# Attention heads of a diffusion trunk: one maximum per query over all keys, unscaled probabilities, sums divided out in the output projection, and no GpSimd work in the heads

## The chip, the cores and the metric

The kernel runs on one core of a Trainium2 chip. Times are device microseconds (us) of one execution. The engines are TensorE (PE; its weight loads are PEld), VectorE (DVE), ScalarE (ACT), GpSimd (POOL) and SyncE (SP, which only issues DMAs here). Each runs its own queue in order and waits on semaphores for the others. PSUM, into which TensorE writes, has eight banks of 128 partitions by 512 fp32 values.

## The reference, cut to what matters

Two layers over 256 context tokens and 1024 latent tokens, each with a token mixer and an MLP. Layer 0 mixes by latent attention with 8 heads, and the change is there:

```python
def mla_attend(q_nope, q_rope, k_nope, k_rope, v):
    scale = (MLA_NOPE + MLA_ROPE) ** -0.5
    s = (jnp.einsum('bqhd,bkhd->bhqk', q_nope, k_nope, preferred_element_type=jnp.float32)
         + jnp.einsum('bqhr,bkr->bhqk', q_rope, k_rope, preferred_element_type=jnp.float32))
    p = jax.nn.softmax(s * scale, axis=-1)
    return jnp.einsum('bhqk,bkhd->bqhd', p.astype(v.dtype), v)
...
    o_lat = jnp.moveaxis(o_lat, 0, 1).reshape(B, S, MLA_HEADS * MLA_V)
    y_lat = o_lat @ w_o
    ...
        o_ctx = mla_attend(q_nope[:, :C], q_rope[:, :C], k_nope[:, :C], k_rope[:, :C], v[:, :C])
        y_ctx = o_ctx.reshape(B, C, MLA_HEADS * MLA_V) @ w_o
```

Latent queries read all 1280 keys, context queries the 256 context keys. Layer 1 (gated linear attention) and the two MLPs are as before.

## The kernel before

Everything is fp32. A product of two fp32 operands is made of three fp32r matmuls: each operand is split into a high part (a cast on ACT, `split`, L203, or `evac`, L575) and the low rest (a subtraction, `sub`, L200, on DVE or POOL); `mm3` (L233 to L235) issues hi*hi, hi*lo, lo*hi.

Tokens are in three blocks: block 0 is the context (256), blocks 1 and 2 are latent (512 each). `heads` runs over 8 heads, and in each over five chunks of 256 queries: two of block 1, two of block 2, one of block 0. For each chunk:

- `scores` (L688) takes two tiles of 128 queries. For each tile it makes the scores against each block of keys in turn (blocks 1, 2 and 0, five matmuls each, L706 to L710), takes that block's maximum on DVE (L711), and exponentiates with that maximum on ACT (L713), with the row sum in the same instruction. The scores against block 0 of both tiles share one PSUM tile, `last`. Then the three maxima are brought together: their minimum (negated maxima, L718), three correction factors by an exponential on ACT (L719), the total (L720), its reciprocal (L722), the factors times it (L723), and each block of probabilities is scaled by its factor (L725): on DVE, but for the first tile's block 1, which is scaled on POOL (`PLAN['sc']`).
- `transposes` (L729) turns the probabilities of the chunk before (TensorE, L738) and splits them. For the pairs of key tiles at 2 and 4 (`PLAN['raw']`) the split goes through an SBUF copy on ACT (L741), so that POOL can do the subtraction; the other three go straight from PSUM, with the subtraction on DVE.
- `attend` multiplies the chunk before that one with the values (L233 to L235, 256 columns each) and stores the result in the DRAM tensor `o_scr`.

Between these, `PLAN` lays out pieces of other work: the next head's keys, queries and rotary parts (`items`), and the modulation vectors (`ada`): `ada_near` as one multiply-and-sum on DVE (L252), `ada_far` as a multiply on POOL (L249) and a sum on ACT (L250). The weights of the heads are split with the subtraction on POOL, and so is one multiply of `rope` (L568).

After the heads `out_proj` multiplies `o_scr` by `w_o`, block 1 first, then 0, then 2, in two halves of the outputs. In the first half each step of k loads a head's `o_scr` rows and splits them with the subtraction on DVE. The residual and norm of the block before run beside it on DVE and ACT (`residual_norm_steps`, L859 and L861).

The builder's scheduler sets each engine's order: it starts from the order of the program text and moves instructions by its own estimate of when they are ready. Loads whose tile is `ada` in the heads are pinned.

Of the kernel before, what the change touches and what calls it, by code (L numbers as in the profile page):

```python
# [14 lines left out]
ALU = mybir.AluOpType  # L15
# [56 lines left out]
 'sc': [(0, 1)],  # L72
 'raw': [4, 2],
# [37 lines left out]
class Trunk:  # L111
    def __init__(self, ctx, tc, I, out, stop=None):
# [35 lines left out]
        self.o_scr = dram("o_scr", [HEADS, P, T])  # L148
        self.hid_scr = [dram(f"hid{l}", [NP, 7, P, 512]) for l in range(2)]
# [409 lines left out]
    def rope(self, raw, b, w):  # L559
        nc, I = self.nc, self.I  # L560
        if b == 0:
            return raw
        c = slice(BLK[b][0] - CTX, BLK[b][0] - CTX + w)
        cos, sin = self.load(I["cos"][:, c], "t"), self.load(I["sin"][:, c], "t")
        sh = self.t(w)
        nc.vector.stream_shuffle(out=sh, in_=raw, mask=SHUF)
        nc.vector.tensor_tensor(out=raw, in0=raw, in1=cos, op=ALU.mult)
        nc.gpsimd.tensor_tensor(out=sh, in0=sh, in1=sin, op=ALU.mult)  # L568
        nc.vector.tensor_tensor(out=raw, in0=raw, in1=sh, op=ALU.add)
        return raw  # L570
# [32 lines left out]
    def hweight(self, h, n):  # L603
        if n not in self.hw:
            self.hw[n] = self.weight(self.I[n][h])
# [33 lines left out]
    def v_items(self, p):  # L639

        self.wv = self.weight(self.I["wv"][p])
# [15 lines left out]
    def heads(self):  # L657
# [3 lines left out]
        for h in range(HEADS):  # L661
            nxt = self.head_items(h + 1) if h + 1 < HEADS else iter(())
            for ci, c in enumerate(((1, 0), (1, 256), (2, 0), (2, 256), (0, 0))):
                pt = self.scores(self.st[h], c)
                for x in PLAN['order'][ci].split():
# [8 lines left out]
                    if x == "ada":  # L674
                        self.ada_some(self.ada_near, PLAN['near'][h][ci], pinned=True)
                        self.ada_some(self.ada_far, PLAN['far'][h][ci], pool=True, pinned=True)
# [9 lines left out]
        self.ada_some(self.ada_far, 1000, pool=True)  # L686

    def scores(self, st, c):  # L688
# [7 lines left out]
        res = []  # L696
        for i in range(2):
            qs = slice(o + i * P, o + i * P + P)
            mx, rs, ex, f = (self.tiny(4) for _ in range(4))
            p = {}  # L700
            for n, kb in enumerate(keys):
# [10 lines left out]
                p[kb] = self.m(w)  # L712
                nc.scalar.activation(p[kb], ps, AF.Exp, bias=mx[:, n:n + 1], accum_out=rs[:, n:n + 1])  # L713
            k = len(keys)
            if k == 1:
                nc.vector.reciprocal(out=f[:, 0:1], in_=rs[:, 0:1])
            else:
                nc.vector.tensor_reduce(out=mx[:, 3:4], in_=mx[:, 0:3], axis=AX.X, op=ALU.min)  # L718
                nc.scalar.activation(ex[:, 0:3], mx[:, 0:3], AF.Exp, bias=mx[:, 3:4], scale=-1.0)  # L719
                nc.vector.tensor_tensor_reduce(out=f[:, 0:3], in0=ex[:, 0:3], in1=rs[:, 0:3], scale=1.0, scalar=0.0,  # L720
                                               op0=ALU.mult, op1=ALU.add, accum_out=f[:, 3:4])
                nc.vector.reciprocal(out=ex[:, 3:4], in_=f[:, 3:4])  # L722
                nc.vector.tensor_scalar(out=f[:, 0:3], in0=ex[:, 0:3], scalar1=ex[:, 3:4], scalar2=None, op0=ALU.mult)  # L723
            for n, kb in enumerate(keys):
                (nc.gpsimd if (i, kb) in PLAN['sc'] else nc.vector).tensor_scalar(out=p[kb], in0=p[kb], scalar1=f[:, n:n + 1], scalar2=None, op0=ALU.mult)  # L725
            res.append(p)
        return res

    def transposes(self, p, c):  # L729
        nc = self.nc  # L730
        res = []
        for j in range(0, 2 if c[0] == 0 else NT, 2):
# [6 lines left out]
            if j in PLAN['raw']:  # L739
                raw = self.t()  # L740
                nc.scalar.copy(raw, ps)  # L741
                res.append(self.msplit(raw))
            else:
                res.append(self.evac(ps, 512))
# [50 lines left out]
    def out_items(self, res, l, b, wname, src, off, xsrc):  # L795
# [867 lines left out]
```

## Time and profile before

| what | value |
|---|---|
| time, median of 3 runs | 2922.29 us (2915.41 to 2922.88) |
| profiled execution | 2915.37 us, span in its trace 2913.6 us |
| TensorE busy | 2746.1 us (94%) |
| VectorE busy | 2313.1 us (79%) |
| ScalarE busy | 1603.9 us (55%) |
| GpSimd busy | 664.0 us (23%) |
| granted TensorE clock over the span | 0.971 |

The span is from the first to the last instruction of the trace. Busy shares are means over stages with different limits, so the parts below look at the heads (182 to 710 us of the span) and at the output projection (710 to 862 us) by themselves. Matmuls overlap in the pipeline: the time of one is longer than the step from one to the next, and the step from start to start is what it costs.

### The profile page before, as it was taken

How to read it: one execution, taken by the hardware profiler on the slowest of the kernel's cores; microseconds unless marked ns; L12 is line 12 of the kernel's file. 1: busy time of each engine (PE TensorE's matmuls, PEld its weight loads, DVE VectorE, ACT ScalarE, POOL GpSimd, SP SyncE). 2: the span in 40 equal slices, each digit the busy share in tenths (PEclk: the TensorE clock that was granted, in tenths of full speed). 3: DMA queues.
4: the chain of work that ended last, by engine and by line, in shares of the span. 5: the costliest groups of instructions: out<-in, count | busy, mean ns of one | idle time of the engine just before them, and what ended most of it. 6: DMA issues, size and time to landing. Idle time of an engine off the chain costs nothing. (4 is left out here: it accounts for less than half of the span.)

```text
span 2913.6 us, 44354 instructions
## 1 busy us (share of the span) xinstructions
PE 2746.1 (94%) x14646; PEld 2354.7 (81%) x14646; DVE 2313.1 (79%) x4331; ACT 1603.9 (55%) x3360; POOL 664.0 (23%) x474
## 2 busy tenths in 40 slices
PE   6799998999989999999999999799888999999997
PEld 4678887898779888888887888688887778888877
DVE  8898899888788887798868673366898898877666
ACT  4566666666466444444545365656665644545443
POOL 5554444422000000000002233356561000000012
PEclk8999999999999999999999999899999999999999
DMA  5222424313646675498735465666586657677454
GB/s 201 77 77 67 129 94 143 101 61 110 230 124 233 197 250 179 163 342 285 245 122 172 166 222 161 202 218 230 189 275 213 224 195 246 203 269 259 146 178 154
DMA packets 319383, 535.47 MB, mean 184 GB/s; under 512 B 33072, under 2 KB 96432, under 8 KB 319152
## 3 DMA queue, kind: packets, MB, share of 16 engines
q1 hardware_dynamic: 313328, 527.39, 54.5%
q10 hardware_dynamic: 5760, 5.25, 0.5%
q8 instruction: 115, 1.88, 0.3%
q14 instruction: 116, 0.95, 0.1%
q0 software_dynamic: 64, 0.00, 0.0%
HBM read 412.18 MB, written 120.32 MB: 183 GB/s over the span
## 5 line engine op out<-in xcount | busy, mean ns | idle before, releaser
L234 PE MATMUL ps<-m,w 128*128 128x512 f32 (+1 forms) x2320 | 897.5, 388 | 13.2 <-DVE m L200 13.2
L233 PE MATMUL ps<-m,w 128*128 128x512 f32 (+1 forms) x2320 | 882.2, 390 | 25.2 <-ACT m L203 14.5
L235 PE MATMUL ps<-m,w 128*128 128x512 f32 (+1 forms) x2320 | 889.7, 387 | 2.1 <-DVE w L200 2.0
L200 POOL TENSOR_TENSOR w<-stg,w 128x512 fp32r<-128x512 f32 (+2 forms) x138 | 194.1, 1409 | 1706.2 <-ACT w L203 1648.3
L233 PEld LDWEIGHTS ps<-m,w 128*128 128x128 f32 x2320 | 439.4, 190 | 118.8 <-ACT m L203 21.8
L234 PEld LDWEIGHTS ps<-m,w 128*128 128x128 f32 x2320 | 442.0, 191 | 103.8 <-DVE m L200 18.3
L235 PEld LDWEIGHTS ps<-m,w 128*128 128x128 f32 x2320 | 440.1, 190 | 91.6 <-DVE w L200 4.4
L203 ACT CAST w<-stg 128x512 fp32r<-128x512 f32 (+2 forms) x510 | 311.1, 615 | 333.0 <-PE ps L234 247.2
L200 DVE TENSOR_TENSOR w<-stg,w 128x512 fp32r<-128x512 f32 x372 | 273.1, 738 | 142.6 <-ACT w L203 127.8
L203 ACT CAST m<-stg 128x512 fp32r<-128x512 f32 x296 | 177.5, 625 | 141.8 <-DMA stg<-hid 123.6
L233 PE MATMUL ps<-m,m 128*128 128x256 f32 (+1 forms) x632 | 187.9, 316 | 28.7 <-ACT m L203 17.7
L200 DVE TENSOR_TENSOR m<-stg,m 128x512 fp32r<-128x512 f32 x244 | 169.1, 706 | 50.0 <-ACT m L203 49.2
L234 PE MATMUL ps<-m,m 128*128 128x256 f32 (+1 forms) x632 | 198.0, 315 | 7.4 <-DVE m L200 4.1
L233 PE MATMUL ps<-c,w 128*128 128x256 f32 (+1 forms) x664 | 186.9, 288 | 15.8 <-ACT c L435 6.3
L235 PE MATMUL ps<-m,m 128*128 128x256 f32 (+1 forms) x632 | 194.9, 310 | 2.4 <-DVE m L426 2.4
L234 PE MATMUL ps<-c,w 128*128 128x256 f32 (+1 forms) x664 | 185.8, 284 | 5.6 <-DVE c L436 3.5
L235 PE MATMUL ps<-c,w 128*128 128x256 f32 (+1 forms) x664 | 185.1, 284 | 0.6 <-DVE w L200 0.6
L233 PEld LDWEIGHTS ps<-m,m 128*128 128x128 f32 x632 | 124.0, 197 | 39.8 <-ACT m L203 19.7
L203 ACT CAST w<-m 128x512 fp32r<-128x512 f32 x128 | 79.2, 622 | 117.1 <-PE ps L234 116.9
L233 PEld LDWEIGHTS ps<-c,w 128*128 128x128 f32 x664 | 125.7, 192 | 21.2 <-ACT c L435 6.7
L888 DVE TENSOR_TENSOR t<-ps,t 128x512 f32<-128x512 f32 x164 | 111.0, 684 | 37.6 <-PE ps L235 27.1
L234 PEld LDWEIGHTS ps<-m,m 128*128 128x128 f32 x632 | 125.2, 198 | 17.6 <-POOL m L200 5.5
(303 smaller groups left out, 5817.5 us busy)
## 6 DMA issues: line engine op xcount, KB each, us to landing
stg<-in_mlp_w SPq DMA_DIRECT2D x256, 256.0 KB, 4.2
stg<-hid SPq DMA_DIRECT2D x227, 256.0 KB, 3.8
hid<-t SPq DMA_DIRECT2D x205, 256.0 KB, 3.3
stg<-in_w SPq DMA_DIRECT2D x182, 256.0 KB, 3.4
ada<-in_adaT SPq DMA_DIRECT2D x88, 512.0 KB, 3.7
stg<-in_adaT SPq DMA_DIRECT2D x112, 256.0 KB, 4.1
stg<-in_gla_wv SPq DMA_DIRECT2D x64, 256.0 KB, 3.6
stg<-in_mla_wo SPq DMA_DIRECT2D x48, 256.0 KB, 4.4
```

The lines of the kernel that those rows point to most:

```text
L200: eng.tensor_tensor(out=out, in0=a, in1=bits(hi), op=ALU.subtract)
L203: self.nc.scalar.copy(hi, src)
L233: mm(ps, lhs[0], rhs[0], start=first, stop=False, skip_group_check=shared)
L234: mm(ps, lhs[0], rhs[1], start=False, stop=False, skip_group_check=shared)
L235: mm(ps, lhs[1], rhs[0], start=False, stop=last, skip_group_check=shared)
L888: eng.tensor_tensor(out=out, in0=a, in1=b, op=op)
```

## The change

`scores` first makes all scores of a query tile, then takes one minimum of the negated maxima, and only then exponentiates all blocks with it. The row sums go into two small constant tiles per head, `parts` and `whole`. Nothing scales the probabilities. A new function `head_sums` adds the sums of a head, takes the reciprocals, turns them with one transpose on TensorE and stores 1280 numbers in a DRAM tensor `f_scr`; it is called for head h - 1 after the second chunk's scores of head h, and for the last head behind all scores. `out_proj` loads, beside each head's `o_scr` rows, the row of `f_scr` broadcast to all partitions, and multiplies on DVE before the split. In the heads the subtractions of the weights and of all transposed probabilities, the multiply of `rope` and the `ada_far` products move from POOL to DVE; the copies for `PLAN['raw']` go.

```diff
@@ rope
-        nc.gpsimd.tensor_tensor(out=sh, in0=sh, in1=sin, op=ALU.mult)
+        nc.vector.tensor_tensor(out=sh, in0=sh, in1=sin, op=ALU.mult)
@@ hweight, v_items
-            self.hw[n] = self.weight(self.I[n][h])
+            self.hw[n] = self.weight(self.I[n][h], self.nc.vector)
-        self.wv = self.weight(self.I["wv"][p])
+        self.wv = self.weight(self.I["wv"][p], self.nc.vector)
@@ heads
+                self.st_of = h
                 pt = self.scores(self.st[h], c)
+                if ci == 1 and h:
+                    self.head_sums(h - 1)
...
-                        self.ada_some(self.ada_far, PLAN['far'][h][ci], pool=True, pinned=True)
+                        self.ada_some(self.ada_far, PLAN['far'][h][ci], pinned=True)
...
         self.attend(*prev)
+        self.head_sums(HEADS - 1)
         self.attend(*later[:2], self.transposes(*later[2:]), later[3])
@@ scores
                 nc.vector.tensor_reduce(out=mx[:, n:n + 1], in_=ps, axis=AX.X, op=ALU.max, negate=True)
-                p[kb] = self.m(w)
-                nc.scalar.activation(p[kb], ps, AF.Exp, bias=mx[:, n:n + 1], accum_out=rs[:, n:n + 1])
...
+                pss.append(ps)
+            top = mx[:, 0:1]
+            if len(keys) > 1:
+                top = mx[:, 3:4]
+                nc.vector.tensor_reduce(out=top, in_=mx[:, 0:3], axis=AX.X, op=ALU.min)
             for n, kb in enumerate(keys):
-                (nc.gpsimd if (i, kb) in PLAN['sc'] else nc.vector).tensor_scalar(out=p[kb], in0=p[kb], scalar1=f[:, n:n + 1], scalar2=None, op0=ALU.mult)
+                p[kb] = self.m(BLK[kb][1])
+                acc = whole[:, j:j + 1] if len(keys) == 1 else parts[:, j - 2, n:n + 1]
+                nc.scalar.activation(p[kb], pss[n], AF.Exp, bias=top, accum_out=acc)
...
+    def head_sums(self, h):
+
+        nc = self.nc
+        parts, whole = self.sums[h % 2]
+        nc.vector.tensor_reduce(out=whole[:, 2:NT], in_=parts, axis=AX.X, op=ALU.add)
+        nc.vector.reciprocal(out=whole, in_=whole)
+        ps = self.ps(P)
+        nc.tensor.transpose(ps[0:NT], whole, self.ident)
+        y = self.t(P)
+        nc.scalar.copy(y[0:NT], ps[0:NT])
+        nc.scalar.dma_start(self.f_scr[h].rearrange("(j t) -> j t", t=P), y[0:NT])
@@ transposes
-            if j in PLAN['raw']:
-                raw = self.t()
-                nc.scalar.copy(raw, ps)
-                res.append(self.msplit(raw))
-            else:
-                res.append(self.evac(ps, 512))
+            res.append(self.evac(ps, 512))
@@ out_items (out_proj)
                 if half == 0:
-                    o.append(self.msplit(self.load(src[k, :, t0 - off:t0 - off + w]), w, self.nc.vector))
+                    x = self.load(src[k, :, t0 - off:t0 - off + w])
+                    if l == 0:
+                        f = self.load(self.f_scr[k:k + 1, t0:t0 + w].to_broadcast([P, w]))
+                        self.tt(self.nc.vector, x, x, f, ALU.mult)
+                    o.append(self.msplit(x, w, self.nc.vector))
```

The change moves instructions in the heads, in the output projection, and in a few places just ahead of them and at the start of the first MLP; behind that every engine's order is the same as before. Two places matter below. Names such as `ps_5380` are tiles with their number; the same tile has another number in the other program.

The first is on ACT, in the last latent chunk of the fifth head (`scores` L713 before, L726 now; L719 are the correction factors, L575 and L741 evacuate transposes). Before:

```order
L713 ACTIVATE c_5743,y_5716<-ps_5714,y_5715 128x256
L713 ACTIVATE m_5726,y_5716<-ps_5719,y_5715 128x512
L713 ACTIVATE m_5735,y_5716<-ps_5728,y_5715 128x512
L719 ACTIVATE y_5717<-y_5715 128x3
L713 ACTIVATE m_5764,y_5754<-ps_5757,y_5753 128x512
L713 ACTIVATE m_5773,y_5754<-ps_5766,y_5753 128x512
L575 CAST m_5830<-ps_5825 128x512
L713 ACTIVATE c_5781,y_5754<-ps_5714,y_5753 128x256
```

Now:

```order
L726 ACTIVATE m_5259,parts_98<-ps_5238,y_5237 128x512
L726 ACTIVATE m_5261,parts_98<-ps_5245,y_5237 128x512
L726 ACTIVATE c_5263,parts_98<-ps_5236,y_5237 128x256
L762 COPY t_5324<-ps_5293 128x256
L764 DMA o_scr<-t_5324 128x256
L726 ACTIVATE m_5287,parts_98<-ps_5266,y_5265 128x512
L726 ACTIVATE m_5289,parts_98<-ps_5273,y_5265 128x512
L726 ACTIVATE c_5291,parts_98<-ps_5236,y_5265 128x256
L575 CAST m_5332<-ps_5327 128x512
L726 ACTIVATE c_5388,whole_99<-ps_5380,y_5381 128x256
```

The three exponentials of a query tile now stand together behind the tile's last maximum, and the evacuation of the first transposes (`m_5332`) and the first exponential of the context chunk (`c_5388`) stand behind the second tile's three.

The second place is on TensorE, in the context chunk that follows in the same head. Its two score groups go into the two halves of one PSUM tile (`ps_5882` before, `ps_5380` now); the rows lead up to the second group. L233 to L235 are `attend`, L738 (L751 now) transposes. Before (ahead of these rows stand the first group and four matmuls of `attend`):

```order
L234 MATMUL ps_5911<-m_5831,m_5186 128x256
L235 MATMUL ps_5911<-m_5830,m_5187 128x256
L738 MATMUL ps_5945<-ident,c_5743 128x128 x2
L738 MATMUL ps_5954<-ident,m_5726 128x128 x2
L738 MATMUL ps_5965<-ident,m_5726 128x128 x2
L738 MATMUL ps_5976<-ident,m_5735 128x128 x2
L738 MATMUL ps_5954<-ident,m_5764 128x128 x2
L738 MATMUL ps_5965<-ident,m_5764 128x128 x2
L738 MATMUL ps_5976<-ident,m_5773 128x128 x2
L233 MATMUL ps_5911<-m_5841,m_5203 128x256
L738 MATMUL ps_5945<-ident,c_5781 128x128 x2
L706 MATMUL ps_5882<-c_4418,c_4976 128x256
```

Now, from the last matmul of the second latent tile's scores on:

```order
L716 MATMUL ps_5236<-k_1174,m_4406 128x256
L751 MATMUL ps_5363<-ident,m_5093 128x128 x2
L751 MATMUL ps_5363<-ident,m_5121 128x128 x2
L712 MATMUL ps_5380<-c_4074,c_4568 128x256
L713 MATMUL ps_5380<-c_4075,c_4568 128x256
L714 MATMUL ps_5380<-c_4074,c_4569 128x256
L715 MATMUL ps_5380<-k_1173,c_4552 128x256
L716 MATMUL ps_5380<-k_1174,c_4552 128x256
L233 MATMUL ps_5399<-m_5332,m_4751 128x256
L751 MATMUL ps_5433<-ident,c_5263 128x128 x2
L751 MATMUL ps_5433<-ident,c_5291 128x128 x2
L712 MATMUL ps_5380<-c_4074,c_4568 128x256
```

Between the two groups of the context chunk stood 7 matmuls of `attend` and 16 transposes; now one matmul of `attend` and four transposes stand there. So it is in heads 1, 3, 5, 7 and 8 of the 8 now; in heads 2, 4 and 6 more stands between.

## Rows read from the trace of the kernel before

**Rows 1.** Busy time of each engine by stage: start:end, length, busy (instructions), clock, DMA.

```profile
182.00:710.00 528.00, 503.26 (x3265) 455.98 (x3264) 466.66 (x1101) 349.46 (x904) 226.10 (x145) 0.97 0.29 94
758.00:780.00 22.00, 22.00 (x174) 21.17 (x173) 18.53 (x34) 13.32 (x25) 0.00 (x0) 1.00 0.50 146
780.00:800.00 20.00, 14.04 (x62) 11.25 (x62) 20.00 (x36) 11.09 (x22) 0.00 (x0) 0.74 0.75 262
```

**Rows 2.** Waits of TensorE in the heads: us in total, times, longest.

```profile
PE ps L233 <- DVE m L200: 5.6, 2, 2.8
PE ps L706 <- DVE m L579: 4.3, 4, 1.9
PE ps L706 <- DVE m L200: 3.2, 1, 3.2
PE ps L738 <- DVE m L725: 2.9, 1, 2.9
```

**Rows 3.** Timeline of DVE around one of these waits: start, us, instruction.

```profile
461.64 2.59 DVE L725 TENSOR_SCALAR m<-m,y 128x512 f32<-128x512 f32 x1
...
465.96 2.07 DVE L723 TENSOR_SCALAR y<-y 128x3 f32<-128x3 f32 x1
```

**Rows 4.** Timeline of POOL in the same stretch.

```profile
459.18 4.76 POOL L249 TENSOR_TENSOR ada<-ada,cs 128x1024 f32<-128x1024 f32 x2 [9.23 <-DVE y L722]
...
465.63 2.38 POOL L249 TENSOR_TENSOR ada<-ada,cs 128x1024 f32<-128x1024 f32 x1
```

**Rows 5.** DVE's groups in the heads: count, busy us, mean ns, idle before.

```profile
L200 DVE TENSOR_TENSOR m<-ps,m 128x512 fp32r<-128x512 f32 x134 | 89.9, 681 | 20.4 <-ACT m L575 15.5 <-PE ps L234 3.5 <-PE ps L235 0.9
L252 DVE CUSTOM_DVE_ANT_0 ada<-ada,cs 128x1024 f32<-128x1024 f32 x48 | 66.0, 1376 | 0.0
L725 DVE TENSOR_SCALAR m<-m,y 128x512 f32<-128x512 f32 x96 | 59.1, 642 | 2.3
L725 DVE TENSOR_SCALAR c<-c,y 128x256 f32<-128x256 f32 x80 | 46.1, 577 | 0.3
L723 DVE TENSOR_SCALAR y<-y 128x3 f32<-128x3 f32 x64 | 31.4, 490 | 0.7
...
L718 DVE TENSOR_REDUCE y<-y 128x1 f32<-128x3 f32 x64 | 9.4, 146 | 0.4
```

**Rows 6.** POOL's groups in the heads.

```profile
L200 POOL TENSOR_TENSOR m<-t,m 128x512 fp32r<-128x512 f32 x64 | 84.9, 1346 | 86.3 <-ACT m L203 45.0 <-PE ps L235 14.8 <-PE ps L738 7.8
L249 POOL TENSOR_TENSOR ada<-ada,cs 128x1024 f32<-128x1024 f32 x24 | 57.4, 2398 | 28.4 <-DMA ada<-in_adaT 15.7 <-DVE y L722 9.2 <-ACT m L203 2.3
...
L200 POOL TENSOR_TENSOR w<-stg,w 128x384 fp32r<-128x384 f32 (+2 forms) x18 | 18.0, 1002 | 23.8 <-ACT w L203 23.8
```

**Rows 7.** Timeline of ACT where it waits for nothing, early in the heads.

```profile
194.28 0.68 ACT L713 ACTIVATE m<-ps,y 128x512 f32<-128x512 f32 x1
...
194.95 0.58 ACT L575 CAST m<-ps 128x512 fp32r<-128x512 f32 x1
195.41 0.49 ACT L713 ACTIVATE c<-ps,y 128x256 f32<-128x256 f32 x1
...
195.87 0.31 ACT L719 ACTIVATE y<-y 128x3 f32<-128x3 f32 x1
```

**Rows 8.** Timeline of TensorE where it waits for nothing, in the heads.

```profile
403.70 1.91 PE L738 MATMUL ps<-ident,m 128*128 128x128 f32 x16
405.36 0.48 PE L706 MATMUL ps<-m,m 128*128 128x512 f32 x1
...
407.76 0.28 PE L706 MATMUL ps<-c,m 128*128 128x256 f32 x1
407.88 0.28 PE L707 MATMUL ps<-c,m 128*128 128x256 f32 x1
```

**Rows 9.** Timeline of DVE in the output projection, block 2's first half.

```profile
790.59 1.28 DVE L200 TENSOR_TENSOR m<-stg,m 128x512 fp32r<-128x512 f32 x2
791.79 0.69 DVE L861 TENSOR_TENSOR m<-m,s 128x512 f32<-128x512 f32 x1
```

More of the change, by code (lines that the diff above doesn't have):

```diff
@@ L71 @@
          [1, 0, 4, 0, 1], [0, 1, 2, 0, 0]],
- 'sc': [(0, 1)],
- 'raw': [4, 2],
  'bufs': {'m': 37, 'c': 16, 'w': 8, 'stg': 1, 't': 5, 'ada': 3},
@@ L148, in __init__ @@
         self.o_scr = dram("o_scr", [HEADS, P, T])
+        self.f_scr = dram("f_scr", [HEADS, T])
+        self.sums = [(const(f"parts{i}", [P, NT - 2, 3]), const(f"whole{i}", [P, NT])) for i in range(2)]
         self.hid_scr = [dram(f"hid{l}", [NP, 7, P, 512]) for l in range(2)]
@@ L683, in heads @@
         self.attend(*prev)
+        self.head_sums(HEADS - 1)
         self.attend(*later[:2], self.transposes(*later[2:]), later[3])
         self.ada_some(self.ada_near, 1000)
-        self.ada_some(self.ada_far, 1000, pool=True)
+        self.ada_some(self.ada_far, 1000)
     def scores(self, st, c):
@@ L696, in scores @@
         res = []
+        parts, whole = self.sums[self.st_of % 2]
         for i in range(2):
+            j = (BLK[qb][0] + o) // P + i
             qs = slice(o + i * P, o + i * P + P)
-            mx, rs, ex, f = (self.tiny(4) for _ in range(4))
-            p = {}
+            mx = self.tiny(4)
+            pss, p = [], {}
             for n, kb in enumerate(keys):
@@ L711, in scores @@
                 nc.vector.tensor_reduce(out=mx[:, n:n + 1], in_=ps, axis=AX.X, op=ALU.max, negate=True)
-                p[kb] = self.m(w)
-                nc.scalar.activation(p[kb], ps, AF.Exp, bias=mx[:, n:n + 1], accum_out=rs[:, n:n + 1])
-            k = len(keys)
-            if k == 1:
-                nc.vector.reciprocal(out=f[:, 0:1], in_=rs[:, 0:1])
-            else:
[L718 to L723, printed above, removed]
+                pss.append(ps)
[3 more added lines that the diff above has]
+                nc.vector.tensor_reduce(out=top, in_=mx[:, 0:3], axis=AX.X, op=ALU.min)
             for n, kb in enumerate(keys):
-                (nc.gpsimd if (i, kb) in PLAN['sc'] else nc.vector).tensor_scalar(out=p[kb], in0=p[kb], scalar1=f[:, n:n + 1], scalar2=None, op0=ALU.mult)
+                p[kb] = self.m(BLK[kb][1])
+                acc = whole[:, j:j + 1] if len(keys) == 1 else parts[:, j - 2, n:n + 1]
+                nc.scalar.activation(p[kb], pss[n], AF.Exp, bias=top, accum_out=acc)
             res.append(p)
         return res
+    def head_sums(self, h):
[8 more added lines that the diff above has]
+        nc.scalar.dma_start(self.f_scr[h].rearrange("(j t) -> j t", t=P), y[0:NT])
     def transposes(self, p, c):
@@ L738, in transposes @@
                     nc.tensor.transpose(ps[:, jj * 256 + i * P:jj * 256 + i * P + P], p[i][b][:, o:o + P], self.ident)
-            if j in PLAN['raw']:
-                raw = self.t()
-                nc.scalar.copy(raw, ps)
-                res.append(self.msplit(raw))
-            else:
-                res.append(self.evac(ps, 512))
+            res.append(self.evac(ps, 512))
         return res
```

## The prediction

> **What bounds the kernel now.** I read first the table of stages, because the change touches two of them alone. In the heads, 182 to 710 us, TensorE is busy 503.3 of 528.0 us and its granted clock is 0.97 [rows 1]. So two things are there to be won: 528.0 - 503.3 = 24.7 us in which TensorE has nothing to run, and what the lower clock costs. A mean of 0.97 between the levels 2.4 and 1.2 GHz means that 6% of the stage ran at the lower one, where each step takes twice its time; 3% of 528 is about 16 us. Together 41 us is the most that this stage can give, since the change takes no matmul away (it adds 8 transposes).
>
> Next the waits of TensorE there: the four longest, 16.0 of the 24.7 us, all end with DVE, at subtractions (L200, L579) and at a scaling (L725) [rows 2]. DVE is busy 466.7 of 528.0 us, 88% [rows 1], which alone is no full engine. The timeline says why it is late. At 461.64 a scaling takes 2.59 us, and at 465.96 a TENSOR_SCALAR on 128x3 numbers takes 2.07 us [rows 3]; each ends with a POOL multiply: the pair that starts at 459.18 ends at 463.94, the next, from 465.63, at 468.01 [rows 4], while the scaling ends at 464.23 and the small one at 468.03. Over the stage the operation on three numbers takes 490 ns in the mean [rows 5], more than three times the reduction of three numbers beside it (146 ns). So DVE stands still behind POOL's longer instructions, a piece of the evacuation comes late, TensorE runs dry, and the clock falls: where TensorE is busy throughout, 758 to 780, it is 1.00, and where it idles for 6 of 20 us, 0.74 [rows 1]. The reader is to see that DVE is short of time in stretches, through POOL.
>
> **What the change takes from the heads.** The scalings on DVE (59.1 + 46.1 us) and the factors (31.4 us) go [rows 5], 136.6 us, and some smaller operations of the old correction with them. To DVE come 64 subtractions, whose POOL copies take 84.9 us there, 24 `ada` products and 18 weight subtractions [rows 6]. At DVE's own prices [rows 5]: 64 x 0.681 = 43.6; 24 x 1.376 = 33.0 at most, as that mean is stretched by POOL too; 18 x 0.681 = 12.3 at most, for most are narrower. With 7 multiplies of `rope` at the same 0.68 (4.8 us) and 8 calls of `head_sums`, bounded by 0.15 and 0.7 us for each of its two operations (2 to 11 us, I take 3, since one has 10 numbers and the other 24 a row), 97 us are added. So DVE loses 40 us or more in a stage that now gives PE its waits, the stretching of the rest goes with POOL, and its share falls under 81%. ACT, at 349.5 us of 528 [rows 1], only loses work (copies, factors, the `ada` sums).
>
> What remains of the 41 us cannot be read from a row. Below, it could be nothing, if other waits end just behind the ones removed; above, all of it. The waits that the trace names end with DVE, and DVE gets both less to do and even durations, so I take four fifths of both parts: 20 us of idle and 12 us of clock, **-32 us**.
>
> **What it adds to the heads.** One maximum over all keys makes the exponentials wait for the tile's last scores. Before, the exponential of a block stood right behind its own maximum; now three stand together, and their PSUM tiles are kept until then. Most chunks have cover: by the new order, with each step at the price of rows 8, TensorE has some 7 us of `attend`, transposes and items between the two tiles' last scores [rows 8], and a tile's maximum, minimum and three exponentials need under 4. The context chunk has not. The prices are: an exponential of 512 columns with its sum 0.67 us (194.28 to 194.95), a cast 0.46 (to 195.41), one of 256 columns 0.46 (to 195.87) [rows 7]; the reduction over three numbers 0.146 [rows 5]; a maximum over 256 columns I take at 0.4, between the 0.146 of that and the 0.681 of an operation twice as wide [rows 5]. From the end of the second latent tile's last scores to the end of the context chunk's first exponential ACT then needs 0.4 + 0.15 + 0.67 + 0.67 + 0.46 + 0.46 + 0.46 = 3.3 us, and the second half of `ps_5380` cannot be written before that, as both halves share one tile. TensorE gets there after 8 transposes at (405.36 - 403.70) / 16 = 0.104 us and 6 matmuls of 256 columns at 0.12 us [rows 8]: 1.6 us. It waits 1.7 to 1.8 us. In this order that is so in five heads of eight: **+9 us**. Before, 2.5 us of matmuls and transposes stood between the two groups alone, and the exponential came at once, so nothing was lost. Below, this is nothing, if TensorE gets there late anyway; above, the same wait at all 40 chunks would be 70 us (it is the second rival).
>
> The 8 transposes of the sums and their copies are below 0.2 us each on TensorE and under other work.
>
> **What it adds to the projection.** 24 multiplies on DVE and 24 loads. A subtraction of 512 columns costs 0.60 us from start to start ((791.79 - 790.59) / 2 [rows 9]); the multiply has the same form, so 16 x 0.60 and 8 of half the width at about 0.33 (an estimate between half and the whole of 0.60) make 12 us. Block 1 comes first, where TensorE has 2.8 us of work for each step (12 steps of 0.23, twice the 0.12 of half the columns [rows 8]) and DVE three operations, 1.8 us: hidden, but for about 1 us at the start, as the second step's factor is now loaded, multiplied, cast and subtracted before TensorE can go on. In block 0 a step is 1.4 us on TensorE and 0.33 + 0.33 + 0.60 on DVE, beside the norm of block 1; DVE is busy 18.5 of 22.0 us there [rows 1], so its 3.5 idle us take the 2.6 us with little over: 1 us. In block 2 there is no cover: from 780 to 800 DVE is busy 20.00 of 20.00 us, TensorE 14.04 at a clock of 0.74 [rows 1]; its 8 x 0.60 = 4.8 us come on top, with about 1 us of lower clock. Sum **+8 us**; 0 if all hides, 14 if nothing does. The loads go on SP's queue between the others; the DMA share there is 0.50 to 0.75 [rows 1], so they have room. The last head's `f_scr` row is only wanted in the eighth step.
>
> **The sum.** -32 + 9 + 8 = -15 us on the profiled execution's 2915.4 gives 2900. That execution stands 6.9 us under the median of the runs shown; against 2922.3 the same difference gives **2907 us**.
>
> **A rule weighed.** The stage's own rows say that DVE loses 40 us net. The Trainium skill, "Perfetto Trace Analysis", section "Optimizing Scalar/DVE Operations", speaks against the direction: where DVE is saturated, it suggests moving work off it, to ScalarE or even GpSimd, and adds that the shared port may make the latter useless. Here DVE is at 88% and the change moves POOL's work to it. Had the scalings stayed, the sum by that rule would be 467 + 97 = 564 us of DVE in a stage of 528, a bound of +36 us.
>
> **The rivals.** First, *all of it is won*: the context chunk's wait is covered by TensorE's own lateness and the stage comes near its matmuls. -38 + 3 + 5 = -30, 2892 us. For it: every wait of rows 2 ends with DVE. Against: the order above has too little between the two groups. Chance 0.17.
>
> Second, *the joint maximum costs as much as POOL did*. Each of the 32 latent chunks loses 0.5 us as well, because exponentials wait behind casts on ACT or PSUM tiles come free late: -15 + 16 = +1, 2923 us. For it: ACT holds the casts of the transposes behind the exponentials. Against: ACT is busy two thirds of the stage. Chance 0.27.
>
> Third, *slower*: scores of two chunks meet in PSUM. A chunk holds five of the eight banks until its second tile's exponentials are done, and the next chunk wants five. If a chunk must wait the 1.3 us that a second tile's maximum, minimum and first exponential take (0.4 + 0.15 + 0.67), 32 x 1.2 = 38 us go: -15 + 38 = +23, 2945 us. It decides from 24 / 32 = 0.75 us for each chunk on, where the loss passes 9 us. Against: TensorE has transposes and `attend` that need no new bank from the held ones. Chance 0.10.
>
> Fourth, *DVE stays the bound* by the moved work, as in the rule: TensorE's waits come of DVE's sheer load in stretches where few scalings stood, so nothing of the 32 us is won, and a tenth of the added 97 us falls into such stretches: +9 + 8 + 10 = +27, 2949 us. Against: the durations of rows 3, which are POOL's. Chance 0.05.
>
> **How the numbers follow.** My forecast has 0.41. A measurement of this kernel tells 0.3%, 8.8 us, from no change. Faster by more than that: nearly all of the forecast (0.38) and of the first rival (0.17): 0.55. Within: the second rival and the rest of the forecast: 0.30. Slower: the third and fourth, 0.15. The forecast's own range is 2897 to 2917. The range reaches from a little past the first rival, 2886, with nearly the whole 41 us, to 2930, past the second rival and a first part of the third, and leaves out no more than 0.2.
>
> **What would show it.** Right: DVE's TENSOR_TENSOR and `ada` operations in the heads keep to one duration; TensorE's idle there falls from 24.7 to under 15 us, and what is left stands at the first matmul of the second context group, released by ACT; the clock of the stage is 0.99. Between the end of the heads and the first MLP's steady run the stage is about 8 us longer, with DVE full in block 2. Wrong: waits of the scores' first matmuls for ACT in every chunk (second or third rival), or DVE idle-free over long stretches of the heads (fourth).

## The result and the profile after

The changed kernel takes 2969.89 us in the median of 4 runs (2962.81 to 2972.21) against 2920.83 us before (4 runs on the same chip), a ratio of 1.0167 with a 95% interval of 1.0144 to 1.0189. The forecast was 2907 us and a gain; the change loses some 49 us. The profiled execution took 2962.81 us, its span is 2961.0 us.

To compare stages of kernels whose heads differ in length, the heads are taken here from the first score matmul to the first matmul of the output projection, and the projection from there to the first store of the next stage's `hid`. First these two stretches before, then after (columns as in [rows 1]: start:end, length, busy of PE, PEld, DVE, ACT and POOL, clock, DMA share, GB/s):

```profile
176.11:716.38 540.27, 512.08 (x3314) 463.17 (x3312) 473.66 (x1108) 356.79 (x919) 232.37 (x150) 0.97 0.29 94
716.38:854.49 138.11, 128.96 (x632) 108.25 (x632) 108.34 (x196) 77.56 (x145) 0.00 (x0) 0.95 0.63 206
```

```profile
176.79:758.44 581.65, 522.86 (x3321) 465.79 (x3319) 394.88 (x818) 285.36 (x750) 2.87 (x2) 0.97 0.27 87
758.44:904.73 146.29, 130.44 (x632) 108.77 (x632) 120.12 (x218) 76.90 (x145) 0.00 (x0) 0.93 0.71 232
```

The heads are 41.4 us longer and the projection 8.2 us. What lies behind both is 2913.6 - 854.5 = 2059.1 us before and 2961.0 - 904.7 = 2056.3 us after. In the heads every engine but TensorE has less to do, DVE 79 us less, and still TensorE's idle time rises from 540.3 - 512.1 = 28.2 us to 58.8 us. So no engine is short of time over the stage; something comes late. The waits of TensorE in the heads, which answer to [rows 2] (total us, times, longest), say who is waited for:

```profile
PE ps L712 <- ACT m L726: 10.5, 9, 1.6
PE ps L233 <- ACT m L726: 9.6, 4, 5.1
PE ps L751 <- ACT m L726: 9.3, 10, 1.6
PE ps L712 <- DVE m L579: 8.2, 3, 3.6
PE ps L233 <- ACT c L726: 5.4, 3, 1.8
```

Before, the four longest ended with DVE. Now four of the five longest end with ACT's exponentials (L726), at the first matmul of a score group (L712), at the transposes (L751) and at other products. ACT itself is busy 285.4 of 581.6 us. Its groups in the heads (columns as in [rows 5]) show what it waits for: DVE's minimum, L722, with 130.9 us of idle time ahead of the wide exponentials.

```profile
L726 ACT ACTIVATE m<-ps,y 128x512 f32<-128x512 f32 x128 | 86.8, 684 | 132.3 <-DVE y L722 130.9 <-ACT t L762 0.4 <-DVE y L717 0.4
```

And DVE's groups there, which answer to [rows 5], show that the minimum in turn stands behind TensorE: 72.8 us of DVE's idle time lie ahead of the maxima over 256 columns, those of the context keys, and end with the last matmul of a score group, L716.

```profile
L252 DVE CUSTOM_DVE_ANT_0 ada<-ada,cs 128x1024 f32<-128x1024 f32 x72 | 87.5, 1216 | 4.4 <-DMA ada<-in_adaT 4.4
...
L717 DVE TENSOR_REDUCE y<-ps 128x1 f32<-128x256 f32 x80 | 33.5, 418 | 82.4 <-PE ps L716 72.8 <-PE ps L751 9.6
...
L722 DVE TENSOR_REDUCE y<-y 128x1 f32<-128x3 f32 x64 | 9.6, 149 | 0.9
```

So TensorE waits for ACT, ACT for DVE, and DVE for TensorE's context scores. The loop can be seen in one chunk. The rows are TensorE's timeline in the last head (start, us, instruction, idle before it). The first row starts the first query tile's context scores, written into the shared tile `last`; the third starts the second query tile's, into the other half of the same tile, 7.1 us later; the last starts the next chunk's scores.

```profile
707.30 0.28 PE L712 MATMUL ps<-c,m 128*128 128x256 f32 x1
...
712.53 0.66 PE L751 MATMUL ps<-ident,m 128*128 128x128 f32 x4 [0.89 <-ACT m L726]
...
714.41 0.36 PE L712 MATMUL ps<-c,m 128*128 128x256 f32 x1
...
716.84 0.50 PE L712 MATMUL ps<-m,m 128*128 128x512 f32 x1 [1.15 <-ACT m L726]
```

ACT's timeline of the same stretch. The first row opens the first tile's exponentials; its third exponential, from 713.04, is the one that reads `last` and ends at 713.51. Only then may the other half be written, and TensorE does so 0.9 us later, at 714.41. The last row opens the second tile's.

```profile
711.70 0.69 ACT L726 ACTIVATE m<-ps,y 128x512 f32<-128x512 f32 x1 [0.77 <-DVE y L722]
...
713.04 0.47 ACT L726 ACTIVATE c<-ps,y 128x256 f32<-128x256 f32 x1
...
716.01 0.69 ACT L726 ACTIVATE m<-ps,y 128x512 f32<-128x512 f32 x1 [1.82 <-DVE y L722]
```

And DVE's: the maximum over the second tile's context scores, then its minimum, which ends 0.03 us ahead of that exponential (the row above that opens the second tile's).

```profile
715.36 0.42 DVE L717 TENSOR_REDUCE y<-ps 128x1 f32<-128x256 f32 x1 [0.97 <-PE ps L716]
715.82 0.16 DVE L722 TENSOR_REDUCE y<-y 128x1 f32<-128x3 f32 x1
```

The second tile's other scores were finished at 710.14 + 0.39 = 710.53 us; all its exponentials stand 5.5 us later, because the context scores among them came last. The next chunk's scores find no free PSUM tile until the first of these ends, at 716.70, and start at 716.84. Over the 32 latent chunks the second context group starts 8.1 us behind the first in the median, before the change 5.2 us (from the starts of the groups' first matmuls in both timelines; the context chunks aside). TensorE is seldom seen waiting at the second group itself: in one of the 32 chunks, for 3.6 us.

```profile
PE ps L712 <- ACT c L726: 3.6, 1, 3.6
```

So the delay is in the order that the builder's scheduler gave TensorE, which puts the second group behind other work, and the waits stand at what follows.

### The profile page after: what moved, and what is told of

Its sections match the earlier page's. It is cut to its first block, busy times and chain, and to the rows that moved or that the text cites. A ratio compares the mean times of both kernels' runs of the same rounds, so it can differ in the third digit from the quotient of the medians.

```text
span 2961.0 us, 43715 instructions
## 1 busy us (share of the span) xinstructions
PE 2748.7 (93%) x14654; PEld 2348.1 (79%) x14654; DVE 2250.6 (76%) x4068; ACT 1533.6 (52%) x3192; POOL 425.5 (14%) x321
## 5 line engine op out<-in xcount | busy, mean ns | idle before, releaser
L234 PE MATMUL ps<-m,w 128*128 128x512 f32 (+1 forms) x2320 | 896.2, 387 | 14.9 <-DVE m L200 14.9
L233 PE MATMUL ps<-m,w 128*128 128x512 f32 (+1 forms) x2320 | 875.7, 388 | 34.7 <-ACT m L203 23.9
L235 PE MATMUL ps<-m,w 128*128 128x512 f32 (+1 forms) x2320 | 889.1, 386 | 1.8 <-DVE w L200 1.8
L233 PEld LDWEIGHTS ps<-m,w 128*128 128x128 f32 x2320 | 436.4, 189 | 128.7 <-ACT m L203 32.0
L235 PEld LDWEIGHTS ps<-m,w 128*128 128x128 f32 x2320 | 438.7, 190 | 90.6 <-DVE w L200 3.6
L200 POOL TENSOR_TENSOR w<-stg,w 128x512 fp32r<-128x512 f32 x115 | 170.7, 1487 | 2260.9 <-ACT w L203 2172.2
L200 DVE TENSOR_TENSOR w<-stg,w 128x512 fp32r<-128x512 f32 (+2 forms) x395 | 284.4, 724 | 144.9 <-ACT w L203 132.8
L203 ACT CAST m<-stg 128x512 fp32r<-128x512 f32 x296 | 177.2, 624 | 146.6 <-DMA stg<-hid 130.9
L233 PE MATMUL ps<-m,m 128*128 128x256 f32 (+1 forms) x632 | 190.8, 321 | 36.0 <-ACT m L203 17.2
L717 DVE TENSOR_REDUCE y<-ps 128x1 f32<-128x512 f32 (+1 forms) x208 | 118.0, 580 | 112.5 <-PE ps L716 102.7
L233 PE MATMUL ps<-c,w 128*128 128x256 f32 (+1 forms) x664 | 186.0, 287 | 16.4 <-ACT c L435 6.9
L235 PE MATMUL ps<-m,m 128*128 128x256 f32 (+1 forms) x632 | 193.5, 307 | 1.8 <-DVE m L426 1.8
L235 PE MATMUL ps<-c,w 128*128 128x256 f32 (+1 forms) x664 | 184.4, 283 | 0.0
L200 DVE TENSOR_TENSOR m<-ps,m 128x512 fp32r<-128x512 f32 x222 | 145.9, 680 | 27.3 <-ACT m L575 16.0
L233 PEld LDWEIGHTS ps<-m,m 128*128 128x128 f32 x632 | 125.8, 200 | 49.1 <-ACT m L203 18.8
L726 ACT ACTIVATE m<-ps,y 128x512 f32<-128x512 f32 x128 | 86.8, 684 | 132.3 <-DVE y L722 130.9
L900 DVE TENSOR_TENSOR t<-ps,t 128x512 f32<-128x512 f32 x164 | 111.0, 684 | 42.1 <-PE ps L235 34.6
```

The source lines that it names most:

```text
L200: eng.tensor_tensor(out=out, in0=a, in1=bits(hi), op=ALU.subtract)
L203: self.nc.scalar.copy(hi, src)
L233: mm(ps, lhs[0], rhs[0], start=first, stop=False, skip_group_check=shared)
L234: mm(ps, lhs[0], rhs[1], start=False, stop=False, skip_group_check=shared)
L235: mm(ps, lhs[1], rhs[0], start=False, stop=last, skip_group_check=shared)
L717: nc.vector.tensor_reduce(out=mx[:, n:n + 1], in_=ps, axis=AX.X, op=ALU.max, negate=True)
```

## The experiments

The reading above is the first theory: the joint maximum is dear *because both query tiles' context scores share a PSUM tile*. The rivals: the joint maximum is dear by itself, as it holds many banks for long; or the loss comes with the work that left POOL, in the evacuation of the transposes or in the `ada` products. All ratios are to the kernel before on the same chip. The row under each is that of its heads, from one profiled execution; the projection's stands beside it where it is used.

**POOL's share back.** All work in the heads that the change moved off POOL goes back there, with its copies and sums on ACT; the joint maximum and the multiplies in the projection stay.

```diff
-        nc.vector.tensor_tensor(out=sh, in0=sh, in1=sin, op=ALU.mult)
+        nc.gpsimd.tensor_tensor(out=sh, in0=sh, in1=sin, op=ALU.mult)
...
-            self.hw[n] = self.weight(self.I[n][h], self.nc.vector)
+            self.hw[n] = self.weight(self.I[n][h])
...
-                        self.ada_some(self.ada_far, PLAN['far'][h][ci], pinned=True)
+                        self.ada_some(self.ada_far, PLAN['far'][h][ci], pool=True, pinned=True)
...
-            res.append(self.evac(ps, 512))
+            if j in (4, 2):
+                raw = self.t()
+                nc.scalar.copy(raw, ps)
+                res.append(self.msplit(raw))
+            else:
+                res.append(self.evac(ps, 512))
```

> The changed kernel with POOL's work in the heads put back (weights' subtractions, ada_far, rope's multiply, the two SBUF copies of transposes); the joint maximum, the unscaled probabilities and the projection's multiply stay. First theory: the joint maximum holds the scores' PSUM tiles and so makes TensorE wait; then this is as slow as the changed kernel or slower, 2960 to 2985 us, as POOL stretches DVE again. Second theory: DVE, which took POOL's work, is late with maxima; then this is back near the kernel before, with the 8 us of the projection: 2922 to 2935 us.

2926.22 us, ratio 1.0035 (1.0021 to 1.0049).

```profile
176.50:712.68 536.18, 505.42 (x3322) 454.29 (x3320) 348.65 (x676) 343.22 (x862) 180.35 (x118) 0.99 0.29 94
```

45 us of the heads come back, though the joint maximum is still there. The time is in the range of the second theory (2922 to 2935 us); the first, in the form in which it was put ahead of this run, gave 2960 to 2985 us and missed. So the two parts of the change act on one another; the loss is not the joint maximum's alone, whatever stands around it.

**Own maxima.** Each block is exponentiated with its own maximum right behind it, as before the change, and the minimum is still taken. The kernel leaves out bringing the blocks together.

```diff
-                pss.append(ps)
+                p[kb] = self.m(w)
+                acc = whole[:, j:j + 1] if len(keys) == 1 else parts[:, j - 2, n:n + 1]
+                nc.scalar.activation(p[kb], ps, AF.Exp, bias=mx[:, n:n + 1], accum_out=acc)
...
-            for n, kb in enumerate(keys):
-                p[kb] = self.m(BLK[kb][1])
-                acc = whole[:, j:j + 1] if len(keys) == 1 else parts[:, j - 2, n:n + 1]
-                nc.scalar.activation(p[kb], pss[n], AF.Exp, bias=top, accum_out=acc)
```

> The changed kernel, but each block of scores is exponentiated with its own maximum right behind it, as before the change, with nothing to bring the blocks together (that part of the computation is left out; the minimum is still taken). DVE and POOL work as in the changed kernel. First theory (the joint maximum makes the wait): the heads fall by 40 us or more, 2890 to 2920 us in all. Second theory (DVE's added work): the wait stays, 2955 to 2970 us.

2897.46 us, ratio 0.9938 (0.9923 to 0.9953).

```profile
177.96:683.66 505.70, 495.00 (x3322) 452.38 (x3320) 395.35 (x818) 293.77 (x750) 2.87 (x2) 1.00 0.31 100
```

The waiting of the exponentials costs 581.6 - 505.7 = 75.9 us in the heads: 48.1 us of TensorE's idle time (58.8 down to 10.7) and 27.9 us of busy time for the same matmuls. The granted clock of the stage is 1.00 here and 0.97 there; by the prediction's own working, 3% of 581.6 us, that makes some 17 of the 27.9 us, and no row separates the rest. Without that wait the rest of the change gains 540.3 - 505.7 = 34.6 us against before.

**Context scores first.** The same maximum and the same shared tile, but the context scores of both query tiles are made ahead of all others, so that both halves are full before anything reads them.

```diff
+        block(0, 0)
+        block(1, 0)
+        top_of(0, 0)
+        top_of(1, 0)
         for i in range(2):
...
+            for kb in keys[:-1]:
+                block(i, kb)
+                top_of(i, kb)
```

> The changed kernel with the scores of both query tiles against the context keys made first, so that the second half of their common PSUM tile no longer waits for the first tile's exponentials; the joint maximum stays. First theory in its narrow form (the common PSUM tile delays the second tile's maximum, and with it the release of its banks): at least half of the heads' 41 us come back, 2920 to 2945 us. In its wide form (any joint maximum holds the banks too long): under a quarter, 2958 to 2972 us. Second theory (DVE): no change, 2965 to 2972 us.

2916.49 us, ratio 1.0003 (0.9992 to 1.0014).

```profile
180.61:700.43 519.82, 499.91 (x3322) 455.10 (x3320) 394.61 (x817) 284.31 (x750) 1.38 (x1) 0.99 0.30 97
```

61.8 us of the 75.9 come back by order alone, more than the narrow form of the theory asked for (its 2920 to 2945 us lie above the time).

**Own tile.** The context scores of each query tile get a PSUM tile of their own. A latent chunk then holds six of the eight banks in place of five.

```diff
-        last = self.ps()
...
-                ps = last[:, i * 256:i * 256 + 256] if kb == 0 else self.ps(w)
+                ps = self.ps(w)
```

> The changed kernel, but each query tile's scores against the context keys have a PSUM tile of their own, so a chunk holds six banks, not five, and the second tile waits for no exponential of the first. Theory A: the heads fall to 515 to 535 us, 2908 to 2930 us. Theory B (a joint maximum holds too many banks, whoever shares them): no faster than the changed kernel, 2965 us or more.

2910.81 us, ratio 0.9978 (0.9964 to 0.9992): well below the changed kernel, and 0.2% below the kernel before, by an interval that just leaves out 1.

```profile
176.74:694.84 518.10, 498.43 (x3322) 454.57 (x3320) 396.06 (x818) 286.76 (x750) 2.92 (x2) 0.99 0.31 98
694.84:842.91 148.07, 131.98 (x632) 109.95 (x632) 120.22 (x219) 76.76 (x145) 0.00 (x0) 0.92 0.70 229
```

63.5 us of the heads come back with *more* banks held, so the number of banks is not what costs. The same place in the last head, in TensorE's timeline (L711 is the first score matmul here): the two context groups, 2.9 us apart, and the next chunk's first scores, which start behind the transposes with no wait.

```profile
650.30 0.28 PE L711 MATMUL ps<-c,m 128*128 128x256 f32 x1
...
653.18 0.28 PE L711 MATMUL ps<-c,m 128*128 128x256 f32 x1
...
655.02 1.91 PE L750 MATMUL ps<-ident,m 128*128 128x128 f32 x16
656.69 0.48 PE L711 MATMUL ps<-m,m 128*128 128x512 f32 x1
```

Over the latent chunks the distance is 2.9 us in the median, and the waits at scores and transposes for an exponential are gone; what is left of them stands at other products, such as these, the longest two of the heads:

```profile
PE ps L233 <- ACT m L725: 6.8, 3, 3.2
PE ps L233 <- ACT c L725: 3.8, 1, 3.8
```

**Own tile in the kernel before.** The same edit, without the change, as a control.

> The kernel before the change with a PSUM tile of its own for each query tile's context scores: the control. Theory A: before the change a block's exponential came right behind its own maximum, so the common tile cost nothing there; 2908 to 2928 us, within 0.3% of before. If the common tile costs the kernel before as well, 2890 to 2905 us, and the gain of the own tile is no part of the change.

2922.00 us, ratio 1.0025 (1.0013 to 1.0037).

```profile
176.64:716.02 539.38, 508.82 (x3313) 458.60 (x3312) 470.64 (x1107) 354.00 (x919) 237.98 (x150) 0.98 0.30 94
```

The heads stay at 539.4 us (540.3 before), though the two context groups of a latent chunk now stand 2.9 us apart in the median and not 5.2. With own maxima they stand 5.5 us apart, in the shared tile, and those heads are the shortest of all (505.7 us). Where each block is exponentiated at once, sharing a tile costs nothing; it is the joint maximum that makes it dear.

**`ada` products on POOL.** Of what left POOL, only the 24 `ada_far` products go back.

```diff
-                        self.ada_some(self.ada_far, PLAN['far'][h][ci], pinned=True)
+                        self.ada_some(self.ada_far, PLAN['far'][h][ci], pool=True, pinned=True)
...
-        self.ada_some(self.ada_far, 1000)
+        self.ada_some(self.ada_far, 1000, pool=True)
```

> The changed kernel with ada_far back on POOL and ACT, nothing else. Theory A (the second tile's scores against the context keys wait for the first tile's exponentials, and the builder puts them later the more subtractions DVE has): the order keeps them 7 us of matmuls behind the first tile's in most chunks, so the heads stay over 560 us, 2945 to 2968 us in all. Theory D (the ada products, 1.2 us each, stand ahead of the minima on DVE): heads near 540, 2922 to 2935 us.

2964.87 us, ratio 1.0166 (1.0141 to 1.0190).

```profile
176.99:747.16 570.17, 514.51 (x3321) 459.05 (x3320) 384.38 (x770) 311.20 (x798) 61.94 (x26) 0.98 0.28 89
```

11 us of the heads in the one profiled execution, and nothing in the time (2962.0 - 895.3 = 2066.7 us lie behind the projection there, 2056.3 after the change). Had the long `ada` products ahead of the minima on DVE been the cause, the heads would have come near 540 us; they make some 11 us.

**Copies on ACT, subtractions on POOL.** Only the evacuation of two of the five transposed tiles goes back to what it was.

```diff
-            res.append(self.evac(ps, 512))
+            if j in (4, 2):
+                raw = self.t()
+                nc.scalar.copy(raw, ps)
+                res.append(self.msplit(raw))
+            else:
+                res.append(self.evac(ps, 512))
```

> The changed kernel with the two SBUF copies of transposes back on ACT and their subtractions on POOL, nothing else. Theory A: the order now has the second tile's context scores 4 us behind the first tile's in most chunks, so the heads fall to 525 to 540 us: 2908 to 2928 us. Theory D: no change, 2960 to 2972 us. Theory E (the transposes' PSUM tiles are held longer without the copy): as theory A here.

2930.17 us, ratio 1.0052 (1.0035 to 1.0068).

```profile
178.33:720.62 542.29, 509.59 (x3321) 459.41 (x3319) 366.19 (x754) 320.24 (x814) 88.38 (x66) 0.98 0.30 93
```

39.4 us of the heads, most of the 45.5 that POOL's whole share gave back. Both numbers lie a little above what the theory of the shared tile gave (525 to 540 us, 2908 to 2928 us).

**Copies on ACT, subtractions on DVE.** As the last, with `self.msplit(raw, 512, nc.vector)`.

> The changed kernel with the two SBUF copies of transposes back on ACT, but their subtractions on DVE. Their PSUM tiles come free after the copy, as before the change; DVE has as much to do as in the changed kernel. Theory A: the order still has most second tiles 7 us or more behind, so the heads stay over 560 us: 2950 to 2972 us. Theory E: as with the subtractions on POOL, 2908 to 2930 us.

2950.38 us, ratio 1.0118 (1.0096 to 1.0141).

```profile
177.40:730.49 553.09, 512.84 (x3321) 459.37 (x3319) 395.61 (x818) 319.30 (x814) 2.90 (x2) 0.98 0.29 92
```

28.6 us of the heads with DVE as full as after the change (395.6 us against 394.9). Theory A gave heads over 560 us and missed these, though its time (2950 to 2972 us) is just met; theory E gave 2908 to 2930 us and missed. So most of what the copies give is not DVE's load; the load may have a part in the rest.

**Own tile and copies.** Both edits at once: do they remove one wait or two?

> Own PSUM tile for each query tile's context scores, and beside it the copies of two of five transposed tiles on ACT with the subtraction on POOL, as before the change. Apart from the change, the own tile took 64 us from the heads (581.6 to 518.1) and the copies 39 us (581.6 to 542.3). Theory A: both remove the same wait, that for the shared tile, so together they give no more than the own tile alone: heads 512 to 522 us, time 2905 to 2917 us. Theory B: the copies help by a way of their own (a PSUM tile of transposes comes free behind one copy on ACT instead of a cast and a subtraction on DVE), so some of the 39 us comes on top: heads under 508 us, 2870 to 2900 us. Theory C: POOL's subtractions stretch DVE again and cost more than they give: heads above 525 us, 2918 us or more.

2920.12 us, ratio 1.0004 (0.9991 to 1.0017).

```profile
176.49:698.04 521.55, 498.45 (x3321) 454.80 (x3319) 371.11 (x754) 318.66 (x814) 89.31 (x66) 0.99 0.30 97
698.04:845.08 147.04, 130.91 (x631) 108.99 (x632) 119.94 (x218) 76.59 (x145) 0.00 (x0) 0.92 0.70 231
```

With the own tile there, the copies give nothing: 521.6 us against 518.1. So they worked on what the own tile removes. A loss through POOL that hides a gain is not seen: DVE's operations keep their time beside POOL's subtractions (`ada` 1232 ns in the mean, 1216 with the own tile alone). Part of it may be the order: the distance between the two context groups of a latent chunk, 8.1 us after the change, is 6.3 us with the copies alone, 5.8 us with all of POOL's share, and 2.9 us here, since the order is made anew for each text. But it is not all: with the copies and the subtractions on DVE the distance is 8.3 us, no shorter than after the change, and still 28.6 us came back. What did that, no run shows. The time, 2920.1, is above the 2905 to 2917 that this theory gave and within that of theory C (2918 or more). In its profiled execution 2918.7 - 845.1 = 2073.6 us lie behind the projection, where it was 2056.3 after the change and 2910.1 - 842.9 = 2067.2 with the own tile alone; the text there is the same, but the scheduler laid it out otherwise in this kernel. So the total says less of the heads than their own rows do.

**No multiplies in the projection.** The loads of `f_scr` and the 24 multiplies are left out, so the sums divide nothing.

```diff
-                    if l == 0:
-                        f = self.load(self.f_scr[k:k + 1, t0:t0 + w].to_broadcast([P, w]))
-                        self.tt(self.nc.vector, x, x, f, ALU.mult)
```

> The changed kernel without the loads of the factors and the multiplies in the output projection (the division by the sums is left out; the sums are still taken and stored). The projection's cost, by both theories 8 us: 2958 to 2965 us, with the heads as in the changed kernel.

2956.92 us, ratio 1.0145 (1.0128 to 1.0162).

```profile
180.82:760.77 579.95, 521.81 (x3322) 464.76 (x3320) 392.89 (x816) 285.06 (x751) 1.38 (x1) 0.97 0.27 87
760.77:898.87 138.10, 128.95 (x632) 108.25 (x632) 108.60 (x196) 77.50 (x145) 0.00 (x0) 0.95 0.63 208
```

The projection is back at 138.1 us, so the multiplies and loads cost 8.2 us there; by the ratios 0.0022 of 2916 us, 6.4 us, with intervals that overlap.

**Multiplies on POOL.** On top of the own tile, those of block 2 alone, then all.

```diff
-                        self.tt(self.nc.vector, x, x, f, ALU.mult)
+                        self.tt(self.nc.gpsimd if b == 2 else self.nc.vector, x, x, f, ALU.mult)
```

> The kernel with a PSUM tile of its own for each query tile's context scores, with the multiplies of the projection's block 2 on POOL, which is idle there (the last run's rows had TensorE idle for 10 us at that block's first matmul, behind DVE's residual). If the projection's 8 us are DVE's multiplies in block 2, half or more come back: 2898 to 2908 us. If they are the loads or the order of the other blocks, nothing: 2908 to 2915 us.

> The same with the multiplies of all three blocks on POOL. 2895 to 2908 us if DVE's multiplies are the cost; 2908 us or more if POOL, at some 1.4 us for each, is late for the first steps of block 1 or makes DVE wait.

2915.26 us (0.9989, 0.9977 to 1.0002) and 2920.28 us (1.0012, 0.9997 to 1.0026). The two projections:

```profile
697.45:853.67 156.22, 132.96 (x632) 110.08 (x632) 120.55 (x211) 76.61 (x145) 16.30 (x8) 0.90 0.67 217
```

```profile
695.91:853.81 157.90, 133.87 (x632) 110.69 (x632) 116.15 (x196) 76.98 (x145) 32.48 (x22) 0.90 0.66 215
```

They are 8 and 10 us longer than the own tile's 148.1, and neither time is in the range given for the case that DVE's multiplies are the cost (2898 to 2908 and 2895 to 2908 us). Eight multiplies take POOL 16.30 us, and what they hold up in the first of the two runs is SP's loads (L213), which wait for them: SP's longest such wait is 5.8 us.

```profile
SPq L213 <- POOL stg L899: 13.5, 6, 5.8
```

It can be followed at block 2. The rows are of POOL, SP and ACT: a multiply that ends at 775.97, the load of `w_o` that goes out behind it, and the cast that waits for that load.

```profile
770.36 5.61 POOL L899 TENSOR_TENSOR stg<-stg,stg 128x512 f32<-128x512 f32 x1 [4.19 <-DMA stg<-f_scr]
...
776.41 0.38 SPq L213 DMA_DIRECT2D stg<-in_mla_wo  x1
...
780.22 0.62 ACT L203 CAST w<-stg 128x512 fp32r<-128x512 f32 x1 [8.64 <-DMA stg<-in_mla_wo]
```

The first cast of block 2 stands behind that one on ACT, and TensorE's wait for it is 14.9 us, where it was 9.9 with the own tile alone.

## Why the prediction was wrong, step by step

**DVE relieved, -32 us: right in size.** The stretched operations are gone: `ada` takes 1216 ns (1376 in [rows 5]) and no operation on three numbers 490 ns any more (the minimum has 149). DVE loses 78.8 us, more than the 40 worked out. With own maxima, where the other step is absent, the heads lose 34.6 us, TensorE idles 10.7 us (forecast: under 15) and the clock is 1.00 (forecast 0.99). Whether the smaller load of DVE or the missing POOL beside it brought this, no run separates.

**The joint maximum, +9 us: this step failed.** It said "Most chunks have cover" and charged a wait to the context chunks alone; measured, it is 75.9 us, or 75.9 / 32 = 2.4 us for each latent chunk if all is put to these. Its own prices were good: a maximum over 256 columns took 0.418 us (0.4 was assumed), a wide exponential 0.684 (0.67). What failed was the reading of the order. The 7 us of other matmuls between the two tiles' last scores were taken as cover for the first tile's exponentials. They are that, but they also put off the second tile's context scores, and now the second tile's whole maximum, all its exponentials, the transposes and the next chunk's scores hang on these. I had seen the shared half as a hazard for the context chunk, and not that each latent chunk has it too. The prediction did work out a bound near what came, 70 us for "the same wait at all 40 chunks", but called it the second rival, which then charged only 0.5 us to each latent chunk, 16 us; so no rival carried it. The third rival (a chance of 0.10, 2945 us) had the sign and the kind of wait, which the prediction also named among its signs of being wrong: the next chunk's scores wait for the second tile's exponentials. It had the cause as five of eight banks held; the own tile, with six, is 63.5 us faster in the heads than the change, so that was not it.

**The projection, +8 us: right in size.** It is 8.2 us. TensorE's longest waits in it, first before, then after the change:

```profile
PE ps L233 <- ACT m L203: 5.8, 3, 2.6
```

```profile
PE ps L233 <- ACT m L203: 15.2, 4, 9.5
PE ps L234 <- DVE m L200: 2.3, 1, 2.3
```

The longest stands at block 2, as forecast, but it goes through ACT's queue: the cast of block 2's first rows stands on ACT behind a step of the norm that waited 5.35 us for DVE, shown here, and DVE had a run of eight operations (L871, 5.38 us from 827.80) ahead of what it waited for.

```profile
835.95 0.63 ACT L297 ACTIVATE m<-m 128x512 f32<-128x512 f32 x1 [5.35 <-DVE m L873]
836.49 0.60 ACT L203 CAST m<-stg 128x512 fp32r<-128x512 f32 x1
```

So the order around DVE's multiplies made it, more than their own 4.8 us; this is read from the rows, and no run separates the two.

**The sum.** Heads -34.6 + 75.9 = +41.3, projection +8.2, all else about -2, is +47.4 us in the spans (2961.0 - 2913.6). Forecast: -32 + 9 + 8 = -15.

**The rule weighed.** The Trainium skill, "Perfetto Trace Analysis", section "Optimizing Scalar/DVE Operations", suggests, where DVE is saturated, moving some of its work to ScalarE or even GpSimd. POOL's share given back took 45 us from the heads, as the rule's direction has it; but with the own tile the same kind of step (two tiles' copies and subtractions off DVE) took nothing, 521.6 against 518.1 us, at a DVE load of 371 in place of 396 us. What looked like load hung on the shared tile.

**Open.** Between the own tile (518.1) and own maxima (505.7) 12.4 us remain, which any joint maximum over three blocks may cost in this order; nothing separates them further. How the 39 us of the copies split between the order, an earlier free PSUM tile and DVE's load is not settled either; the two runs with copies differ by some 11 us (553.1 - 542.3), in which DVE's load and the order (8.3 and 6.3 us between the groups) both changed.

## What to carry to other kernels

When a reduction is made joint over several PSUM tiles, follow the tile that is written last: everything behind the reduction waits for it, so the work between its producer and the others is delay and not cover. Two groups in the halves of one tile are in a chain as soon as the first reader waits for a joint result; give each a tile, or fill both halves first, even if more banks are held. And when moving work to another engine helps, test it once more with the suspected wait removed, before it is put down to load.

## What was not expected of the hardware

Behind the projection the kernel with the own tile issues the same instructions as the changed kernel on TensorE, VectorE and ScalarE, in the same order but for some neighbours that changed places near the start, and yet took 2067.2 us there in its profiled execution against 2056.3: 10.9 us, more than the 8.8 us (0.3%) by which the prediction set apart a gain from no change. 7.7 of these are busy time of TensorE for the same matmuls (1975.4 against 1967.7 us), and the mean granted clock of the stretch is 0.978 against 0.983. So most of the difference goes with the clock; why less of it was granted there, no run shows.

Gains of a stage are therefore read in the stage. The heads repeat well: the three kernels with the own tile that differ in the projection alone have 518.1, 519.3 and 518.3 us, and the changed kernel with and without the multiplies 581.6 and 580.0. The version with the own tile is 22.2 us faster than before in the heads and 10.0 us slower in the projection, but only 0.2% faster in the time (0.9964 to 0.9992).
